# Softmax cross-entropy on one core: PSUM accumulators, new load sizes and one first transfer in place of two

## The chip, the core and the metric

The kernel runs on one core of one Trainium2 chip. The metric is the device time of one execution in microseconds; a kernel is timed in several executions and the median counts. A core has five engines with an instruction queue each: TensorE (PE, matmuls), VectorE (DVE), ScalarE (ACT, activation functions), GpSimd (POOL) and SyncE (SP, which here only issues transfers). Transfers between main memory and the on-chip memory SBUF are carried out by 16 DMA engines. Matmuls write to a second on-chip memory, PSUM.

## What is computed

For 256 rows of 32000 logits, the loss of each row against its label:

```python
log_probs = logits - np.max(logits, axis=-1, keepdims=True)
log_probs = log_probs - np.log(np.sum(np.exp(log_probs), axis=-1, keepdims=True))
return np.array([-log_probs[i, labels[i]] for i in range(batch)]).astype(np.float32)
```

Logits are float32 (32.77 MB in all), labels int32, the output 256 float32. The kernel leaves the maximum out and computes log(sum(exp(x)) * exp(-x[label])), which is the same number.

## The kernel before

**Layout.** Partition p of the 128 holds logits rows 2p and 2p + 1 one after the other, so it reads 64000 columns; "row 0" and "row 1" below are those two halves. The columns are cut into 14 loads, numbered 0 to 13, with the widths in `CHUNKS` (line 18). Loads 0 to 5 have SBUF buffers of their own (`SLOTS`, line 22), load 6 reuses load 2's, and loads 7 to 13 lie side by side in load 1's (`x_tail`, line 86). So load 6 is issued only when exp 2 is done, and loads 7 to 13 only when exp 1 is done; they stand behind load 6 in SP's queue.

**Loads.** All are issued from SP by `load` (line 110), one transfer each, except load 0, which is two transfers: the even partitions, then the odd ones (lines 114 to 116). `begin_first_load_before_barrier` (line 30) takes the first two of SP's transfers out of the kernel's body and puts them ahead of the barrier that all engines pass at the start of the program.

**Exps.** `exps` (line 120) has ScalarE compute exp of a load in place, with the sum over the columns as a second output. In the profile that is an ACTIVATE and, after it, an ACTIVATION_READ_ACCUMULATOR that writes the sum. The load in which row 0 ends (`turn`, load 3) is done in two pieces. The sums go to columns of `parts[r]` (SBUF, one column for each piece), that of load 13 to `s_last`.

**Labels.** A transfer issued from POOL brings the labels into `lbl` (line 145), POOL adds the rows' offsets (line 150), and two indirect transfers gather the logit of each label into `g` (line 152). ScalarE computes `eg` = exp(-g) between exp 2 and exp 3 (line 167), and VectorE scales the identity by it into two diagonal matrices `diag` (line 169).

**Reduction.** For each half, VectorE sums `parts[r]` into `sums` (lines 173 and 181), and a matmul of that column with `diag[r]` multiplies by exp(-g) and turns the 128 partitions into one row in PSUM, `lane[r]` (lines 174 and 182). For row 1 a second matmul adds `s_last` (line 184). A float32 matmul is two passes in the profile. ScalarE takes the logarithm (`log_row`, line 135), for row 0 after exp 4, for row 1 at the end, and one transfer stores 256 results.

**Products that nobody reads.** After exp 8 (`WARM_FROM`) TensorE computes 12 matmuls into `warm` (lines 177 to 180) that are not used for the result.

The order of the instructions on each engine is the order of the program's text (`manual_schedule`, line 140). Semaphores between engines are put in by the framework; beyond data dependences, a transfer also waits until an earlier one that used the same semaphore has landed.

Of the kernel before, what the change touches and what calls it, by code (L numbers as in the profile page):

```python
# [9 lines left out]
P = 128  # L10
ROWS = 2
F32 = mybir.dt.float32
# [3 lines left out]


CHUNKS = [
    1024, 15104, 12672, 8960, 7136, 4992, 3872,
    2848, 2144, 1600, 1216, 992, 800, 640,  # L20
]
SLOTS = [0, 1, 2, 3, 4, 5, 2]
TAIL = len(SLOTS)
TAIL_SLOT = 1

WARM_FROM = 8
WARM = 12


def begin_first_load_before_barrier(nc):  # L30


    main, body = nc.m.functions[0].blocks[:2]
    rest = list(body.instructions)
    first = [i for i in rest if i.engine == mybir.EngineType.SP and i.opcode == "DMACopy"][:2]
    for i in first:
        rest.remove(i)
    head = list(main.instructions)
    at = next(
        k for k, i in enumerate(head) if i.engine == mybir.EngineType.SP and i.opcode == "Drain"  # L40
    )
    head[at:at] = first
    main.instructions = head
    body.instructions = rest


@with_exitstack
def kernel(
    ctx: ExitStack,
    tc: tile.TileContext,  # L50
    logits: bass.AP,
    labels: bass.AP,
    out: bass.AP,
):
    nc = tc.nc
    nc.at_finalize(begin_first_load_before_barrier)
    B, C = logits.shape
    assert B == P * ROWS and sum(CHUNKS) == ROWS * C


    flat = logits.rearrange("(p r) c -> p (r c)", r=ROWS)


    pieces = []
    starts = []
    at = 0
    for n in CHUNKS:
        starts.append(at)
        cuts = [at] + [c for c in range(C, ROWS * C, C) if at < c < at + n] + [at + n]
        pieces.append([(a, b, a // C) for a, b in zip(cuts, cuts[1:])])  # L70
        at += n
    last = len(CHUNKS) - 1

    turn = next(i for i in range(len(CHUNKS)) if starts[i] + CHUNKS[i] >= C)

    big = ctx.enter_context(tc.tile_pool(name="big", bufs=1))
    small = ctx.enter_context(tc.tile_pool(name="small", bufs=1))
    psum = ctx.enter_context(tc.tile_pool(name="psum", bufs=1, space=bass.MemoryType.PSUM))

    width = {}  # L80
    for i, s in enumerate(SLOTS):
        width[s] = max(width.get(s, 0), CHUNKS[i])
    tiles = []
    for i, s in enumerate(SLOTS):
        tiles.append((big.tile([P, width[s]], F32, name=f"x{i}", tag=f"slot{s}"), starts[i]))
    tail = big.tile([P, width[TAIL_SLOT]], F32, name="x_tail", tag=f"slot{TAIL_SLOT}")
    assert sum(CHUNKS[TAIL:]) <= width[TAIL_SLOT]
    tiles += [(tail, starts[TAIL])] * (len(CHUNKS) - TAIL)

    n_of = [sum(1 for ps in pieces[:-1] for q in ps if q[2] == r) for r in range(ROWS)]  # L90
    parts = [small.tile([P, n_of[r]], F32, name=f"parts{r}") for r in range(ROWS)]
    s_last = small.tile([P, 1], F32, name="s_last")
    res = small.tile([1, ROWS * P], F32, name="res")
    sums = small.tile([P, ROWS], F32, name="sums")
    ident = small.tile([P, P], F32, name="ident")
    diag = [small.tile([P, P], F32, name=f"diag{r}") for r in range(ROWS)]
    lane = [psum.tile([1, P], F32, name=f"lane{r}") for r in range(ROWS)]
    warm = psum.tile([1, P], F32, name="warm")
    lbl = small.tile([P, 2 * ROWS], I32, name="lbl")
    idx = small.tile([P, ROWS], I32, name="idx")  # L100
    g = small.tile([P, ROWS], F32, name="g")
    eg = small.tile([P, ROWS], F32, name="eg")

    nc.scalar.preload_act_table_set("natural_log_exp_and_others")  # L104

    lbl_words = dataclasses.replace(
        labels.tensor, shape=[labels.tensor.shape[0] * 2], dtype=I32
    )

    def load(i):  # L110
        t, base = tiles[i]
        a, b = starts[i], starts[i] + CHUNKS[i]

        step = 2 if i == 0 else 1
        for p in range(step):
            nc.sync.dma_start(out=t[p:P:step, a - base:b - base], in_=flat[p:P:step, a:b])  # L116

    seen = [0] * ROWS

    def exps(i):  # L120
        t, base = tiles[i]
        for a, b, r in pieces[i]:
            if i == last:
                acc = s_last[:, :]
            else:
                acc = parts[r][:, seen[r]:seen[r] + 1]
                seen[r] += 1
            nc.scalar.activation(  # L128
                out=t[:, a - base:b - base],
                in_=t[:, a - base:b - base],  # L130
                func=AF.Exp,
                accum_out=acc,
            )

    def log_row(r):
        nc.scalar.activation(  # L136
            out=res[0:1, r:ROWS * P:ROWS], in_=lane[r][:, :], func=AF.Ln
        )

    with tc.manual_schedule():  # L140
        first = len(set(SLOTS))
        for i in range(first):
            load(i)

        nc.gpsimd.dma_start(  # L145
            out=lbl[:, :], in_=bass.AP(tensor=lbl_words, offset=0, ap=[[2 * ROWS, P], [1, 2 * ROWS]])
        )
        nc.gpsimd.iota(out=idx[:, :], pattern=[[C, ROWS]], base=0, channel_multiplier=ROWS * C)  # L148
        make_identity(nc, ident[:, :])
        nc.gpsimd.tensor_add(out=idx[:, :], in0=idx[:, :], in1=lbl[:, 0:2 * ROWS:2])  # L150
        for r in range(ROWS):
            nc.gpsimd.indirect_dma_start(  # L152
                out=g[:, r:r + 1],
                out_offset=None,
                in_=logits[:, :],
                in_offset=bass.IndirectOffsetOnAxis(ap=idx[:, r:r + 1], axis=1),
            )


        done = 0  # L160
        for i in range(first, len(CHUNKS)):
            slot = SLOTS[i] if i < TAIL else TAIL_SLOT
            while done <= SLOTS[:first].index(slot):
                exps(done)
                done += 1
            load(i)
        nc.scalar.activation(out=eg[:, :], in_=g[:, :], func=AF.Exp, scale=-1.0)  # L167
        for r in range(ROWS):
            nc.vector.tensor_scalar_mul(diag[r][:, :], ident[:, :], eg[:, r:r + 1])  # L169
        for i in range(done, last):  # L170
            exps(i)
            if i == turn:
                nc.vector.reduce_sum(out=sums[:, 0:1], in_=parts[0][:, :], axis=mybir.AxisListType.X)  # L173
                nc.tensor.matmul(lane[0][:, :], sums[:, 0:1], diag[0][:, :], start=True, stop=True)  # L174
            if i == turn + 1:
                log_row(0)
            if i == WARM_FROM:
                col = parts[1][:, seen[1] - 1:seen[1]]
                for _ in range(WARM):
                    nc.tensor.matmul(warm[:, :], col, diag[0][:, :], start=True, stop=True)  # L180
        nc.vector.reduce_sum(out=sums[:, 1:2], in_=parts[1][:, :], axis=mybir.AxisListType.X)  # L181
        nc.tensor.matmul(lane[1][:, :], sums[:, 1:2], diag[1][:, :], start=True, stop=False)  # L182
        exps(last)
        nc.tensor.matmul(lane[1][:, :], s_last[:, :], diag[1][:, :], start=False, stop=True)  # L184
        log_row(1)
        nc.sync.dma_start(
            out=out.rearrange("(a n) -> a n", a=2), in_=res[0:1, :].rearrange("o (a n) -> o a n", a=2)
        )
# [30 lines left out]
```

## Time and profile before

| what | value |
|---|---|
| median of 3 runs | 87.37 us (87.28 to 87.47) |
| the profiled execution's own time | 87.28 us |
| its span, first to last instruction | 85.5 us |
| ACT busy | 58.4 us (68% of the span) |
| PE busy | 6.1 us (7%) |
| POOL, DVE busy | 3.7 us, 0.8 us |
| read from main memory | 32.77 MB, 383 GB/s over the span |
| ACT idle until a load landed | 22.8 us in 4 waits, longest 19.8 |
| exp 1 (15104 columns) | starts at 24.64, takes 12.79 us |
| exp 13 (640 columns) | starts at 81.87, takes 0.72 us |
| last matmul pair, Ln, store issued | 82.73, 83.15, 83.45 |

Times are microseconds from the span's start. The profile gives the busy time of each engine, the chain of work that ended last, what each idle engine waited for, and for each transfer the time from its issue to its landing, that is until the last of its parts had arrived. The trace also has the records of the DMA engines' packets. A line number is that of the kernel's text.

### The profile page before, as it was taken

What the parts mean: (1) busy time and instruction counts of PE and PEld (TensorE: products, weight loads), DVE (VectorE), ACT (ScalarE), POOL (GpSimd) and SP (SyncE); (2) the same over time, 40 slices, a digit from 0 to 9 for tenths busy, and PEclk for the clock granted to TensorE, in tenths of its full rate; (3) what the DMA queues carried; (4) which work ended last, traced back from release to release, by engine and by line L of the source; (5) the groups of instructions that cost most, each with busy time, mean ns of one, the idle gap of its engine ahead of it and who ended that gap; (6) DMA issues with size and microseconds to landing.
All of it is one profiled execution on the core that took longest, in us unless ns stands there. A gap on an engine that the chain in (4) does not pass through costs nothing.

```text
span 85.5 us, 177 instructions
## 1 busy us (share of the span) xinstructions
PE 6.1 (7%) x30; PEld 3.0 (4%) x30; DVE 0.8 (1%) x4; ACT 58.4 (68%) x34; POOL 3.7 (4%) x11
## 2 busy tenths in 40 slices
PE   0000000000000000000000000200000000007980
PEld 0000000000000000000000000000000000004530
DVE  0000000000000000000000020000000000000000
ACT  1720000000049999954999999998999999999970
POOL 0600005400000000000000000000000000000000
PEclk9999999999999999999999999999999999999999
DMA  3996999999999999999989999999999999999300
GB/s 73 427 424 255 425 424 452 424 453 424 393 427 427 498 403 403 403 434 419 470 369 453 435 428 427 427 394 430 437 415 442 407 427 414 411 410 405 148 0 0
DMA packets 2131, 32.77 MB, mean 383 GB/s; under 512 B 338, under 2 KB 339, under 8 KB 1107
## 3 DMA queue, kind: packets, MB, share of 16 engines
q1 hardware_dynamic: 2034, 32.77, 90.9%
q0 software_dynamic: 96, 0.00, 0.4%
q14 instruction: 1, 0.00, 0.0%
HBM read 32.77 MB, written 0.00 MB: 383 GB/s over the span
## 4 chain that ended last, share of the span: by engine, by line
DMA 44%; ACT 38%; issue 13%; PE 0%; SPq 0%; another core or an unknown queue 0%
DMA x<-in_logits_dram 44%; ACT x L128 26%; ACT x_tail L128 12%; ACT res L136 1%; PE lane L184 0%; SPq L116 0%; ACT eg L167 0%
## 5 line engine op out<-in xcount | busy, mean ns | idle before, releaser
L128 ACT ACTIVATE x<-x 128x1024 f32<-128x1024 f32 (+7 forms) x8 | 46.4, 5794 | 22.8 <-DMA x<-in_logits_dram 22.8
L128 ACT ACTIVATE x_tail<-x_tail 128x2848 f32<-128x2848 f32 (+6 forms) x7 | 9.8, 1404 | 0.0
L180 PE MATMUL warm<-diag,parts 128*1 128x128 f32 x24 | 4.9, 392 | 23.2 <-ACT x_tail L128 23.2
L174 PE MATMUL lane<-diag,sums 128*1 128x128 f32 x2 | 0.6, 394 | 53.7 <-DVE sums L173 53.7
L180 PEld LDWEIGHTS warm<-diag,parts 128*1 128x1 f32 x24 | 2.8, 118 | 25.5 <-ACT x_tail L128 23.7
L104 ACT ACT_TABLE_LOAD x1 | 1.3, 1283 | 1.8 <-PEq L203 1.8
L152 POOL DMA_INDIRECT g<-in_logits_dram,idx x2 | 2.0, 995 | 0.6 <-issue 0.3
L174 PEld LDWEIGHTS lane<-diag,sums 128*1 128x1 f32 x2 | 0.1, 80 | 53.7 <-DVE sums L173 53.7
L128 ACT ACTIVATION_READ_ACCUMULATOR x<-x 128x1 f32 x8 | 1.5, 186 | 0.0
L128 ACT ACTIVATION_READ_ACCUMULATOR x_tail<-x_tail 128x1 f32 x7 | 1.3, 185 | 0.0
L169 DVE TENSOR_SCALAR diag<-ident,eg 128x128 f32<-128x128 f32 x2 | 0.5, 284 | 50.7 <-ACT eg L167 50.7
L136 ACT ACTIVATE res<-lane 1x128 f32<-1x128 f32 x2 | 0.5, 264 | 0.5 <-PE lane L184 0.5
L145 POOL DMA_DIRECT2D lbl<-in_labels_dram x1 | 0.7, 712 | 1.9 <-POOLq L203 1.9
L150 POOL TENSOR_TENSOR idx<-idx,lbl 128x2 int32<-128x2 int32 x1 | 0.2, 193 | 9.5 <-DMA lbl<-in_labels_dram 9.5
L181 DVE TENSOR_REDUCE sums<-parts 128x1 f32<-128x10 f32 x1 | 0.2, 164 | 28.4 <-ACT x_tail L128 28.4
L184 PE MATMUL lane<-diag,s_last 128*1 128x128 f32 x2 | 0.4, 270 | 0.1
L182 PE MATMUL lane<-diag,sums 128*1 128x128 f32 x2 | 0.4, 270 | 0.0
masks.py:199 POOL TENSOR_SCALAR_AFFINE_SELECT ident<-ident 128x128 f32<-128x128 f32 x1 | 0.3, 292 | 0.1
masks.py:197 POOL MEMSET ident<- 128x128 f32 x1 | 0.2, 232 | 0.0
L167 ACT ACTIVATE eg<-g 128x2 f32<-128x2 f32 x1 | 0.2, 187 | 0.0
L173 DVE TENSOR_REDUCE sums<-parts 128x1 f32<-128x4 f32 x1 | 0.2, 157 | 2.3 <-ACT x L128 2.3
L148 POOL IOTA idx<- 128x2 int32 x1 | 0.2, 162 | 0.1
(6 smaller groups left out, 0.6 us busy)
## 6 DMA issues: line engine op xcount, KB each, us to landing
x<-in_logits_dram SPq DMA_DIRECT2D x1, 7552.0 KB, 22.8
x<-in_logits_dram SPq DMA_DIRECT2D x1, 6336.0 KB, 37.4
x<-in_logits_dram SPq DMA_DIRECT2D x1, 4480.0 KB, 47.5
x<-in_logits_dram SPq DMA_DIRECT2D x1, 3568.0 KB, 55.5
x<-in_logits_dram SPq DMA_DIRECT2D x1, 2496.0 KB, 60.5
x<-in_logits_dram SPq DMA_DIRECT2D x1, 1936.0 KB
x_tail<-in_logits_dram SPq DMA_DIRECT2D x1, 1424.0 KB, 21.7
x_tail<-in_logits_dram SPq DMA_DIRECT2D x1, 1072.0 KB, 23.8
```

The source lines that it names most:

```text
L104: nc.scalar.preload_act_table_set("natural_log_exp_and_others")
L128: nc.scalar.activation(out=t[:, a - base:b - base], in_=t[:, a - base:b - base], func=AF.Exp, accum_out=acc,)
L136: nc.scalar.activation(out=res[0:1, r:ROWS * P:ROWS], in_=lane[r][:, :], func=AF.Ln)
L145: nc.gpsimd.dma_start(out=lbl[:, :], in_=bass.AP(tensor=lbl_words, offset=0, ap=[[2 * ROWS, P], [1, 2 * ROWS]]))
L148: nc.gpsimd.iota(out=idx[:, :], pattern=[[C, ROWS]], base=0, channel_multiplier=ROWS * C)
L150: nc.gpsimd.tensor_add(out=idx[:, :], in0=idx[:, :], in1=lbl[:, 0:2 * ROWS:2])
L152: nc.gpsimd.indirect_dma_start(out=g[:, r:r + 1], out_offset=None, in_=logits[:, :], in_offset=bass.IndirectOffsetOnAxis(ap=idx[:, r:r + 1 ...
L169: nc.vector.tensor_scalar_mul(diag[r][:, :], ident[:, :], eg[:, r:r + 1])
L174: nc.tensor.matmul(lane[0][:, :], sums[:, 0:1], diag[0][:, :], start=True, stop=True)
L180: nc.tensor.matmul(warm[:, :], col, diag[0][:, :], start=True, stop=True)
L182: nc.tensor.matmul(lane[1][:, :], sums[:, 1:2], diag[1][:, :], start=True, stop=False)
L184: nc.tensor.matmul(lane[1][:, :], s_last[:, :], diag[1][:, :], start=False, stop=True)
```

## The change

Five things are changed.

1. Load 0 is one transfer of 128 partitions again, and only this one is moved ahead of the barrier.
2. The widths of the loads are others; their number and their sum stay.
3. The sums of exps 7 to 12 go to six PSUM tiles `far` of one column each. After each of these exps VectorE copies the column to an SBUF tile `near`, and a matmul adds it into `lane[1]`. The reduction of `parts[1]` now covers the loads up to 6 and stands after exp 6. The two `lane` rows share one PSUM tile.
4. The 12 unread matmuls stand after exp 7 and take as their column one of load 7's exps in place of a sum.
5. The labels' transfer is issued from ScalarE's queue, behind the load of the function table and ahead of exp 0.

```diff
--- before.py
+++ after.py
@@ -16,15 +16,17 @@


 CHUNKS = [
-    1024, 15104, 12672, 8960, 7136, 4992, 3872,
-    2848, 2144, 1600, 1216, 992, 800, 640,
+    1024, 16384, 12512, 9024, 6656, 5088, 3744,
+    2688, 2016, 1504, 1120, 864, 736, 640,
 ]
 SLOTS = [0, 1, 2, 3, 4, 5, 2]
 TAIL = len(SLOTS)
 TAIL_SLOT = 1

-WARM_FROM = 8
+WARM_FROM = 7
 WARM = 12
+
+IN_PSUM = range(7, 13)


 def begin_first_load_before_barrier(nc):
@@ -32,14 +34,13 @@

     main, body = nc.m.functions[0].blocks[:2]
     rest = list(body.instructions)
-    first = [i for i in rest if i.engine == mybir.EngineType.SP and i.opcode == "DMACopy"][:2]
-    for i in first:
-        rest.remove(i)
+    first = next(i for i in rest if i.engine == mybir.EngineType.SP and i.opcode == "DMACopy")
+    rest.remove(first)
     head = list(main.instructions)
     at = next(
         k for k, i in enumerate(head) if i.engine == mybir.EngineType.SP and i.opcode == "Drain"
     )
-    head[at:at] = first
+    head.insert(at, first)
     main.instructions = head
     body.instructions = rest

@@ -87,14 +88,20 @@
     assert sum(CHUNKS[TAIL:]) <= width[TAIL_SLOT]
     tiles += [(tail, starts[TAIL])] * (len(CHUNKS) - TAIL)

-    n_of = [sum(1 for ps in pieces[:-1] for q in ps if q[2] == r) for r in range(ROWS)]
+    n_of = [
+        sum(1 for ps in pieces[:IN_PSUM[0]] for q in ps if q[2] == r) for r in range(ROWS)
+    ]
+    assert all(len(pieces[i]) == 1 for i in IN_PSUM) and turn < IN_PSUM[0]
+    far = {i: psum.tile([P, 1], F32, name=f"far{i}") for i in IN_PSUM}
+    near = {i: small.tile([P, 1], F32, name=f"near{i}") for i in IN_PSUM}
     parts = [small.tile([P, n_of[r]], F32, name=f"parts{r}") for r in range(ROWS)]
     s_last = small.tile([P, 1], F32, name="s_last")
     res = small.tile([1, ROWS * P], F32, name="res")
     sums = small.tile([P, ROWS], F32, name="sums")
     ident = small.tile([P, P], F32, name="ident")
     diag = [small.tile([P, P], F32, name=f"diag{r}") for r in range(ROWS)]
-    lane = [psum.tile([1, P], F32, name=f"lane{r}") for r in range(ROWS)]
+    lane_tile = psum.tile([1, ROWS * P], F32, name="lane")
+    lane = [lane_tile[:, r * P:(r + 1) * P] for r in range(ROWS)]
     warm = psum.tile([1, P], F32, name="warm")
     lbl = small.tile([P, 2 * ROWS], I32, name="lbl")
     idx = small.tile([P, ROWS], I32, name="idx")
@@ -110,10 +117,7 @@
     def load(i):
         t, base = tiles[i]
         a, b = starts[i], starts[i] + CHUNKS[i]
-
-        step = 2 if i == 0 else 1
-        for p in range(step):
-            nc.sync.dma_start(out=t[p:P:step, a - base:b - base], in_=flat[p:P:step, a:b])
+        nc.sync.dma_start(out=t[:, a - base:b - base], in_=flat[:, a:b])

     seen = [0] * ROWS

@@ -122,6 +126,8 @@
         for a, b, r in pieces[i]:
             if i == last:
                 acc = s_last[:, :]
+            elif i in IN_PSUM:
+                acc = far[i][:, :]
             else:
                 acc = parts[r][:, seen[r]:seen[r] + 1]
                 seen[r] += 1
@@ -142,7 +148,7 @@
         for i in range(first):
             load(i)

-        nc.gpsimd.dma_start(
+        nc.scalar.dma_start(
             out=lbl[:, :], in_=bass.AP(tensor=lbl_words, offset=0, ap=[[2 * ROWS, P], [1, 2 * ROWS]])
         )
         nc.gpsimd.iota(out=idx[:, :], pattern=[[C, ROWS]], base=0, channel_multiplier=ROWS * C)
@@ -174,12 +180,17 @@
                 nc.tensor.matmul(lane[0][:, :], sums[:, 0:1], diag[0][:, :], start=True, stop=True)
             if i == turn + 1:
                 log_row(0)
+            if i == IN_PSUM[0] - 1:
+                nc.vector.reduce_sum(out=sums[:, 1:2], in_=parts[1][:, :], axis=mybir.AxisListType.X)
+                nc.tensor.matmul(lane[1][:, :], sums[:, 1:2], diag[1][:, :], start=True, stop=False)
+            if i in IN_PSUM:
+                nc.vector.tensor_copy(out=near[i][:, :], in_=far[i][:, :])
+                nc.tensor.matmul(lane[1][:, :], near[i][:, :], diag[1][:, :], start=False, stop=False)
             if i == WARM_FROM:
-                col = parts[1][:, seen[1] - 1:seen[1]]
+                at = starts[i] - tiles[i][1]
+                col = tiles[i][0][:, at:at + 1]
                 for _ in range(WARM):
                     nc.tensor.matmul(warm[:, :], col, diag[0][:, :], start=True, stop=True)
-        nc.vector.reduce_sum(out=sums[:, 1:2], in_=parts[1][:, :], axis=mybir.AxisListType.X)
-        nc.tensor.matmul(lane[1][:, :], sums[:, 1:2], diag[1][:, :], start=True, stop=False)
         exps(last)
         nc.tensor.matmul(lane[1][:, :], s_last[:, :], diag[1][:, :], start=False, stop=True)
         log_row(1)
```

## The prediction

> **What bounds the kernel now.** I read the chain that ended last in order of time, then the transfers with their time to landing, the DMA rate by stage, and last the order of instructions near both ends.
>
> ```profile
> 2.25 37.36 DMA x<-in_logits_dram
> 39.62 0.02 issue
> ...
> 72.85 9.84 ACT x_tail L128 x14
> 82.69 0.04 issue
> 82.73 0.39 PE lane L184 x2
> ```
>
> The first 39.62 us are DMA, the rest is ScalarE without a pause worth naming: it looks like two bounds. The landings say it is one.
>
> ```profile
> x<-in_logits_dram SPq DMA_DIRECT2D x1, 7552.0 KB, 22.8
> x<-in_logits_dram SPq DMA_DIRECT2D x2, 256.0 KB, 3.0
> x_tail<-in_logits_dram SPq DMA_DIRECT2D x1, 320.0 KB, 17.0
> ```
>
> Load 1 was issued at 1.83 and landed at 1.83 + 22.8 = 24.62; load 13 was issued at 64.60 and landed at 81.60. Exp 13 starts at 81.87, only 0.27 after its data. So the end is the **DMA stream's end plus 0.27 us of ScalarE's lag**, plus a fixed tail (last exp, matmul pair, Ln, store).
>
> The stream is regular once it runs. Load 2 took 39.62 - 24.62 = 15.00 for 12672 columns and load 3 took 10.62 for 8960, so 4.38/3712 = 1.180 ns a column; from load 1 to load 13, 56.98 us for 47872 columns in 12 loads leave about 0.037 a load. It is not regular at its start:
>
> ```profile
> 4.00:6.00 2.00, 0.00 (x0) 0.00 (x0) 0.00 (x0) 0.83 (x2) 0.00 (x0) 1.00 0.84 302
> 6.00:8.00 2.00, 0.00 (x0) 0.00 (x0) 0.00 (x0) 0.00 (x0) 0.00 (x0) 1.00 0.98 393
> ...
> 26.00:28.00 2.00, 0.00 (x0) 0.00 (x0) 0.00 (x0) 2.00 (x1) 0.00 (x0) 1.00 0.99 431
> ```
>
> The last column is GB/s: 302 and 393 early, 431 later. The trace's packet records (start, length, bytes of each) show why. The 16 DMA engines finish load 0 at about 3.2; seven start on load 1 at once (3.08 to 3.27), the other nine at 3.87 to **4.95**. From then on each moves at its own steady pace, so load 1 lands on the first engine at 22.32 and on the last at 24.62, load 13 at 79.21 and 81.60: the late engine sets every landing. Whatever that engine gains at the start, the end gains.
>
> **Part 1, load 0 as one transfer, one issue ahead of the barrier.**
>
> ```profile
> 0.60 0.58 SPq L116 DMA_DIRECT2D x<-in_logits_dram  x1
> 1.83 0.37 SPq L116 DMA_DIRECT2D x<-in_logits_dram  x1
> ```
>
> SP reaches the barrier after its second issue. Without it the barrier, the table load and load 1's issue all come 0.60 earlier, load 1's at 1.23. Against that, one transfer has 128 rows to hand out. The packets show first rows on the engines from 1.34 to 1.90 for the first 64 rows, 0.56, and for load 1's 128 rows, which can start 1.34 after its issue (3.17), until 4.95, 1.78. If load 0's 128 rows go at the first pace (1.12), they are out by 2.46, before load 1 can start (1.23 + 1.34 = 2.57): load 1's last engine starts 0.60 earlier. At the second pace load 0 is out at 3.12 and load 1's last engine starts at 4.90: gain 0.05. Both rows describe the same unit and I have nothing to prefer one, so **-0.33**, bounds -0.60 and -0.05. Exp 0 may move either way: exp 1 waits 19.8 us.
>
> **Part 2, the labels' transfer from POOL's queue to ACT's.** On ACT it stands behind the table load and ahead of exp 0; SP's issues take 0.33 to 0.58, and exp 0's delay is covered as above. Inside the DMA engines it replaces one 128-byte packet each, 0.015 to 0.633 long, 0.58 on the latest engine (the next latest, 0.08 ahead at landing, had 0.31). Each row on SP's queue is one packet in the trace, so ACT's queue would put 8 packets of 16 bytes on each engine, between rows of load 1. The nearest row is the gather's 32-byte packets: 0.015 each between two rows, so 8 x 0.017 = 0.14. The two latest engines would gain 0.44 and 0.17, the landing 0.17 + 0.08 = 0.25. Other end: one of the eight waits the full 0.633, plus seven short ones, 0.75, a loss of 0.17. ACT's rows may also be handed out beside load 1's (rival 2), so I take **-0.15**. The labels may land as late as load 1, about 25; the index add, two gathers (1.0 each, 9.7 to landing) end near 37, and eg is read at 50.4: 13 us of cover, after which each microsecond costs one.
>
> The Trainium skill, "DMA: Bandwidth & Descriptors", section Specifications, speaks against 16-byte rows: under 512 B a transfer is read, modified and written. The 15 ns packets show no such price; no run here shows it for the labels.
>
> **Part 3, sizes and PSUM accumulators.** An exp costs, start to next start, (12789 - 10762)/2432 = 0.8335 ns a column plus 0.187: 72.76 to 75.32 for 2848. Of the 0.187, 0.093 is the accumulator's read that the next exp doesn't overlap.
>
> ```profile
> 64.75 0.19 ACT L128 ACTIVATION_READ_ACCUMULATOR x<-x 128x1 f32 x1
> 64.84 0.26 ACT L136 ACTIVATE res<-lane 1x128 f32<-1x128 f32 x1
> 65.00 4.34 ACT L128 ACTIVATE x<-x 128x4992 f32<-128x4992 f32 x1
> ```
>
> No instruction of the trace makes ScalarE write PSUM. The nearest reads it: Ln holds ScalarE 0.156 for 128 columns, so 0.049 beyond them, where the exp of 2 columns in SBUF (eg) holds it 0.094. That is 0.044 less, which I take for each of the six: 0.143 in place of 0.187. Bounds: the whole read hidden (0.094), or its full 0.185 exposed (0.28).
>
> Through load 6 exps 3 to 6 start within 0.04 of their landings (exp 3: 2080 + 6944 columns, 7.52 + 0.37 = 7.89 against load 4's 6656 x 1.181 + 0.037 = 7.90). Exp 6 needs 3.12 + 0.187 = 3.31 for a load of 3.21, so exp 7 starts 0.115 late. From there ScalarE needs 8928 x 0.8333 = 7.44 plus six overheads; loads 8 to 13 take 6880 x 1.181 + 0.22 = 8.35. At 0.143: 8.30, exp 13 is 0.07 late, against 0.27 now: **-0.20**. At 0.187: 0.33 late, +0.06. At 0.094: never under 0.02, -0.25. At 0.28: 0.89 late, +0.62. The columns moved into loads 0 and 1 cost the stream nothing: the total stays 64000.
>
> **Part 4, the sums on VectorE and TensorE.** Six copies and pairs of matmuls are spread behind exps 7 to 12. Only the last is near the path. Today the reduce (0.164, at 82.00) and its pair (0.38) end at 82.59, and the last pair waits for exp 13 until 82.73: 0.14 spare. A copy of one PSUM column instead of the reduce costs between nothing and the 128-column scaling's 0.28, +0.12: hidden, price 0. The unread products start after exp 7, about 75.3 instead of 77.44, at 0.213 a pass; passes went to 0.109 at 81.45 to 81.66, some 4.1 us after the first. So the change comes at about 79.4, and the 26 passes end near 80.1, before exp 12. Where the clock stays slow, the last pair costs 0.58 (line 174) and not 0.38.
>
> The Trainium skill, "TensorE: Matmul & The Clock Gate", section Part 1, adds that the activity window of about 3.4 us runs freely: an estimate from that page has the fast clock 3.4 to 6.8 us after the first product, 80.9 to 84.3 before and 78.7 to 82.1 after, so that some runs before end slow and hardly any after. It would take up to another 0.2 from the median; the profiled run, already fast at 82.73, shows nothing of it, and it is not in the sum.
>
> **Slot waits.** Load 6 still waits for exp 2, now near 51.1, with loads 4 and 5 queued to 65. Loads 12 and 13 wait for an earlier landing (now 58.67 and 64.58); after, load 5's at the latest, with 14 us of data queued. Free.
>
> **Sum.** 87.28 (span 85.5, 1.8 around it) - 0.33 - 0.15 - 0.20 = 86.60. The median of the runs, 87.37, lies 0.09 above the profiled one, so **86.7**.
>
> **Rivals.**
> 1. *The start gives nothing.* The stagger of one 128-row transfer eats the earlier barrier, and labels cost what they did: 87.37 - 0.20 = 87.17; with no gain from PSUM 87.43. For it: load 1's own stagger of 1.78. So 87.0 to 87.5.
> 2. *Slower: labels and load 1 share the handing out.* ACT's issue follows the barrier within 0.1 of SP's. If the 128 label rows are dealt alternately with load 1's, load 1's last engine starts up to 1.78 later: 4.95 - 0.33 + 1.78 = 6.40, +1.45; with -0.15 - 0.20, 88.5; half shared, 87.6. It decides from a last start after 5.3. Against it: load 1 is issued first.
> 3. *PSUM is dearer.* At 0.28, +0.62 - 0.48: 87.5. Against it: Ln's row.
>
> Chances: forecast 0.55 (86.2 to 87.1), rival 1 0.22, rival 2 0.15, rival 3 0.08. The best of all bounds, -0.60 - 0.25 - 0.25, gives 86.3; the range 86.1 to 87.8 leaves out the upper part of rival 2. About 0.2% (0.17 us) is what a measurement can tell from no change: faster 0.62 (the forecast and a third of rival 1), same 0.17 (half of rival 1 and of rival 3), slower 0.21 (rival 2 and the rest).
>
> **What would show it.** Load 1 issued near 1.23; its landing near 24.62 + 1.51 (1280 columns) - 0.48 = 25.65; accumulator reads into PSUM with the next exp some 0.05 behind them; exp 13 within 0.1 of its landing. A load 1 landing after 26.3 makes the forecast wrong, as does exp 13 over 0.4 late.

## The result and the profile after

The kernel after takes **84.42 us** (median of 6 runs, 84.13 to 84.65) against 87.33 (6 runs, 87.08 to 87.71) for the kernel before on the same chip: a ratio of 0.9665, 95% interval 0.9636 to 0.9693. The forecast was 86.7 with a range from 86.1 to 87.8: the sign was right, the gain is 2.9 us and not 0.6. The profiled execution took 84.65 us with a span of 82.9. (Here and below, ratios leave out disturbed runs, which the medians contain; where the kernel before had some on its chip, the two differ, by 1.3% at most, in e12.)

The chain that ended last, of the kernel after (start, length, what):

```profile
1.18 37.38 DMA x<-in_logits_dram
38.56 0.02 issue
...
71.01 9.07 ACT x_tail L134 x14
80.08 0.04 issue
80.13 0.39 PE lane L195 x2
```

It has the shape of before: DMA first, then ScalarE without a pause. DMA ends 1.06 earlier (38.56 against 39.62) although it has brought 1120 more columns by then (loads 0 to 2: 29920 against 28800, 1.32 us at 1.180 ns a column). The last matmul pair is 2.60 earlier. So 2.4 of the 2.6 are there before 39 us, and the end of the kernel, where most of the change was made, adds little.

The transfers of the kernel after (kind, count, KB where given, us from issue to landing):

```profile
x<-in_logits_dram SPq DMA_DIRECT2D x1, 22.8
x_tail<-in_logits_dram SPq DMA_DIRECT2D x1, 320.0 KB, 16.0
lbl<-in_labels_dram ACTq DMA_DIRECT2D x1, 2.0 KB, 22.9
```

The first line is load 1. It takes 22.8, as before, for 1280 columns more. Its issue and that of load 0, on SP's own rows of the kernel after:

```profile
0.00 0.40 SPq L120 DMA_DIRECT2D x<-in_logits_dram  x1
0.80 0.33 SPq L120 DMA_DIRECT2D x<-in_logits_dram  x1
```

Load 1 is issued at 0.80, 1.03 earlier than before and 0.43 earlier than forecast: one issue (0.55) and its gap (0.05) are gone, the issue that is left takes 0.40 in place of 0.58, and SP's drain behind it takes 0.12 in place of 0.37. It lands at 23.57; forecast was 25.65. With the columns' 1.51 us set aside the landing has gained 24.62 + 1.51 - 23.57 = 2.56.

The packet records of the DMA engines say where. They don't name the engine, but each row of load 1 that begins within 0.003 us of the end of an earlier packet follows it on its engine; the others begin after an idle time.

| | before | after |
|---|---|---|
| engines that go from load 0 to load 1 within 0.003 us | 7 of 16 | **16 of 16** |
| the others stand idle at least | 0.58 to 1.66 us | none |
| latest first row of load 1 | 4.95 | 3.66 |
| first rows take (the steady pace of this row length) | 2.4 to 3.0 (2.23) | 2.42 to 2.53 (2.42) |
| longest packet of the labels | 0.63 | 0.009 |

Idle time is counted here from the latest end of any packet of load 0, so it is a least value.

How the 2.56 splits can't be read off exactly, since the engines have no names. Over all 16, the first row of load 1 begins 0.78 earlier on average (3.88 to 3.10; the latest 1.29 earlier), and the rows of load 1 run over their steady pace by 0.07 an engine in place of 0.82. The labels come on top: on the two engines that end load 1 last, before, their packets take 0.58 and 0.60. If packets that join without a gap are followed, the engine that starts at 4.95 is not one of these two: its last row ends at 23.62, theirs at 24.10 and 24.17.

One view misled me. The DMA rate in two-microsecond windows, for the kernel after (last column GB/s):

```profile
2.00:4.00 2.00, 0.00 (x0) 0.00 (x0) 0.00 (x0) 0.08 (x1) 0.00 (x0) 1.00 1.73 719
4.00:6.00 2.00, 0.00 (x0) 0.00 (x0) 0.00 (x0) 1.15 (x2) 0.00 (x0) 1.00 1.14 492
6.00:8.00 2.00, 0.00 (x0) 0.00 (x0) 0.00 (x0) 0.00 (x0) 0.00 (x0) 1.00 0.92 393
```

719 is far above the steady 431, and 393 at 6 to 8 stands here too, though nothing is slow: the view counts a packet whole in the window in which it begins, and a row takes 2.42 us, longer than the window. With each packet's bytes spread over its own time, the kernel after moves 432 and 433 GB/s at 4 to 6 and 6 to 8, and the kernel before 313 and 376. So the prediction read its 302 and 393 rightly: the start of before is slow. Twelve-microsecond windows err less, though the busy share of 1.12 shows that they still do; the first twelve microseconds of before, then of after (spread in the same way, 334 and 399):

```profile
1.00:13.00 12.00, 0.00 (x0) 0.00 (x0) 0.00 (x0) 2.43 (x3) 1.31 (x4) 1.00 0.97 366
```

```profile
1.00:13.00 12.00, 0.00 (x0) 0.00 (x0) 0.00 (x0) 2.23 (x3) 0.46 (x3) 1.00 1.12 459
```

### The profile page after: what moved, and what is told of

It reads as the page before. It is cut to its first block, busy times and chain, and to the rows that moved or that the text cites. A ratio compares the mean times of both kernels' runs of the same rounds, so it can differ in the third digit from the quotient of the medians.

```text
span 82.9 us, 204 instructions
## 1 busy us (share of the span) xinstructions
PE 7.5 (9%) x42; PEld 3.7 (4%) x42; DVE 1.7 (2%) x10; ACT 58.1 (70%) x34; POOL 3.0 (4%) x10
## 4 chain that ended last, share of the span: by engine, by line
DMA 45%; ACT 38%; issue 13%; PE 0%; SPq 0%
DMA x<-in_logits_dram 45%; ACT x L134 26%; ACT x_tail L134 11%; ACT res L142 1%; PE lane L195 0%; SPq L120 0%; ACT eg L173 0%
## 5 line engine op out<-in xcount | busy, mean ns | idle before, releaser
L134 ACT ACTIVATE x<-x 128x1024 f32<-128x1024 f32 (+7 forms) x8 | 46.9, 5866 | 21.4 <-DMA x<-in_logits_dram 21.4
L134 ACT ACTIVATE x_tail<-x_tail 128x2688 f32<-128x2688 f32 (+6 forms) x7 | 9.1, 1346 | 0.0
L193 PE MATMUL warm<-diag,x_tail 128*1 128x128 f32 x24 | 4.3, 359 | 0.0
L193 PEld LDWEIGHTS warm<-diag,x_tail 128*1 128x1 f32 x24 | 2.7, 112 | 1.6
L188 PE MATMUL lane<-diag,near 128*1 128x128 f32 x12 | 2.0, 292 | 2.2 <-DVE near L187 2.2
L187 DVE COPY near<-far 128x1 f32<-128x1 f32 x6 | 0.9, 158 | 7.4 <-ACT x_tail L134 7.4
L188 PEld LDWEIGHTS lane<-diag,near 128*1 128x1 f32 x12 | 0.8, 82 | 3.3 <-DVE near L187 3.1
```

Source lines behind the costliest of these rows:

```text
L134: nc.scalar.activation(out=t[:, a - base:b - base], in_=t[:, a - base:b - base], func=AF.Exp, accum_out=acc,)
L187: nc.vector.tensor_copy(out=near[i][:, :], in_=far[i][:, :])
L188: nc.tensor.matmul(lane[1][:, :], near[i][:, :], diag[1][:, :], start=False, stop=False)
```

## The experiments

All ratios are to the kernel before on the same chip; the runs were spread over several chips. "At once" is the number of DMA engines whose first row of load 1 begins within 0.05 us of the latest end of a packet before it, so at most that many go on at once. "Idle" is the range of the others' time since that end, so they stand idle at least that long. "Latest" is the latest first row of load 1. All three are of one profiled execution; that of e1 (85.65) is the slowest of its runs, that of e11 (86.54) the fastest. On the chip of e9 to e12 the kernel before itself took 85.81 to 88.19, so small differences there say little.

| run | median (runs) | ratio, 95% | load 1 issued | at once | idle | latest |
|---|---|---|---|---|---|---|
| before | 87.33 (6) | 1 | 1.83 | 7 | 0.58-1.66 | 4.95 |
| after | 84.42 (6) | 0.9665, 0.9636-0.9693 | 0.80 | 16 | - | 3.66 |
| e1 | 84.71 (5) | 0.9716, 0.9639-0.9793 | 0.80 | 15 | 0.33 | 3.57 |
| e2 | 87.38 (10) | 1.0039, 0.9998-1.008 | 1.83 | 5 | 0.06-1.90 | 5.23 |
| e3 | 87.23 (10) | 0.9939, 0.9892-0.9986 | 1.83 | 6 | 0.58-2.35 | 5.71 |
| e4 | 84.57 (4) | 0.9712, 0.9615-0.9809 | 0.80 | 16 | - | 3.29 |
| e5 | 87.96 (10) | 1.005, 1.0015-1.0085 | 1.23 | 9 | 1.01-2.02 | 5.59 |
| e6 | 85.94 (4) | 0.9852, 0.9791-0.9913 | 1.77 | 3 | 0.09-1.21 | 4.40 |
| e7 | 84.43 (6) | 0.9658, 0.9618-0.9698 | 0.81 | 16 | - | 3.32 |
| e8 | 84.41 (6) | 0.9662, 0.9621-0.9703 | 0.81 | 16 | - | 3.43 |
| e9 | 87.21 (10) | 1.0083, 1.0022-1.0144 | 1.27 | 8 | 0.55-1.99 | 5.03 |
| e10 | 86.78 (10) | 1.0023, 0.9967-1.0078 | 1.84 | 12 | 0.22-1.00 | 4.66 |
| e11 | 87.23 (4) | 1.0126, 0.9977-1.0276 | 1.83 | 6 | 0.11-1.26 | 4.56 |
| e12 | 84.25 (4) | 0.9807, 0.9638-0.9976 | 0.80 | 16 | - | 3.12 |
| e13 | 86.75 (4) | 0.9895, 0.9829-0.9962 | 1.35 | 10 | 0.85-1.42 | 4.81 |
| e14 | 86.91 (4) | not given | 1.20 | 11 | 1.24-1.99 | 5.22 |
| e15 | 86.84 (10) | 0.9905, 0.9872-0.9938 | 1.28 | 13 | 0.70-0.80 | 4.54 |
| e16 | 87.53 (10) | 0.997, 0.9928-1.0012 | 1.48 | 6 | 0.22-2.22 | 5.66 |
| e17 | 86.20 (4) | 0.9864, 0.978-0.9949 | 1.83 | 13 | 0.09-0.63 | 5.52 |
| e18 | 85.23 (4) | 0.9748, 0.9672-0.9824 | 1.35 | 16 | - | 4.70 |

### One part at a time

**e1**, the kernel before with load 0 as one transfer, alone ahead of the barrier:

```diff
-    ... i.opcode == "DMACopy"][:2]
+    ... i.opcode == "DMACopy"][:1]
-        step = 2 if i == 0 else 1
+        step = 1
```

> The kernel before with load 0 as one transfer and one issue ahead of the barrier, nothing else. Theory T1 (issue): load 1 is issued near 0.8 in place of 1.83, its late rows are hidden behind load 0, and it lands 1.0 to 1.5 us earlier (23.1 to 23.6): 86.0. Theory T2 (labels): what holds load 1 back is POOL's transfer of the labels right behind the barrier, which is still there: late and slow first rows stay, 0.0 to 0.3 us gained, 87.1. Theory T3 (row size): load 1's rows of 60416 bytes are dealt out slower than rows of 65536 bytes and stay so: 0.0 to 0.3 us gained, 87.1.

It gives 84.71, 2.4 of the 2.9 us, with the old sizes, sums in SBUF and the labels on POOL. The labels' longest packet falls from 0.63 to 0.13 without being moved.

**e2**, before with the labels' transfer on `nc.scalar` in place of `nc.gpsimd`:

> The kernel before with the labels' transfer issued from ScalarE's queue, nothing else. T2: load 1's first rows take 2.23 us in place of 2.4 to 3.0 and the labels' packets 0.1 in place of 0.6 on the latest engine, load 1 lands 1.0 to 1.3 us earlier: 86.2. T1 and T3: only the labels' packets get cheaper, 0.2 to 0.6 us: 86.9.

**e3**, before with the `CHUNKS` of after:

> The kernel before with the widths of the kernel after, nothing else. T3: load 1 (1280 columns more, worth 1.51 us) lands near 25.0 in place of 26.1 and the end comes 1.1 us earlier: 86.3. T1 and T2: load 1 lands at 26.1, the stream ends as before, ScalarE's lag at exp 13 is 0.33 in place of 0.27: 87.4.

**e4**, after with the labels' transfer back on `nc.gpsimd`:

> The kernel after with the labels' transfer issued from POOL's queue again, nothing else. T2: 1.0 to 1.3 us are lost again: 85.6. T1 and T3: 0.2 to 0.6 us lost through the labels' packets: 84.8.

The labels cost nothing that these runs can tell on either queue, alone (e2) or with the rest (e4, whose interval is 1% wide on either side). In e4 their longest packet is 0.78, longer than before, and the time is still 84.57. The sizes alone give between 0.1 and 1.1% by the ratio, with medians that differ by 0.13 the other way: at most a fraction of what e1 gives.

**e7**, after with the accumulators in SBUF:

```diff
-    far = {i: psum.tile([P, 1], F32, name=f"far{i}") for i in IN_PSUM}
+    far = {i: small.tile([P, 1], F32, name=f"far{i}") for i in IN_PSUM}
```

> The kernel after with the six accumulators in SBUF, copies and matmuls as they are. By the prediction's term an exp then takes 0.187 and not 0.143 beyond its columns, exp 13 starts 0.33 after its landing in place of 0.12: +0.2 us, 84.6. If the shorter step from exp to exp is given back by a longer last accumulator read (0.23 in the kernel after against 0.185), +0.15 or less. Rival: the PSUM accumulators are what made the kernel faster: +1 us or more.

84.43: no gain shows in the time, but a ratio's interval of 0.4% (0.35 us) can't tell 0.2 from nothing, and the kernel after was not timed beside it. What PSUM does shows in the rows of exp 7, then of exp 13, in the kernel after:

```profile
70.92 2.43 ACT L134 ACTIVATE x_tail<-x_tail 128x2688 f32<-128x2688 f32 x1
73.25 0.15 ACT L134 ACTIVATION_READ_ACCUMULATOR x_tail<-x_tail 128x1 f32 x1
73.30 1.87 ACT L134 ACTIVATE x_tail<-x_tail 128x2016 f32<-128x2016 f32 x1
...
79.22 0.77 ACT L134 ACTIVATE x_tail<-x_tail 128x640 f32<-128x640 f32 x1
79.84 0.23 ACT L134 ACTIVATION_READ_ACCUMULATOR x_tail<-x_tail 128x1 f32 x1
80.13 0.38 PE L195 MATMUL lane<-diag,s_last 128*1 128x128 f32 x2
```

The next exp starts 0.05 behind the start of the read into PSUM (73.25 to 73.30), as forecast; from exp to exp that is 0.143 beyond the columns in place of 0.187. But the reads lengthen with each exp, from 0.150 (exp 7) to 0.192 (exp 12), and the last one, into SBUF, takes 0.230. In e7 it takes 0.18:

```profile
79.10 0.72 ACT L134 ACTIVATE x_tail<-x_tail 128x640 f32<-128x640 f32 x1
79.73 0.18 ACT L134 ACTIVATION_READ_ACCUMULATOR x_tail<-x_tail 128x1 f32 x1
```

With the sums in SBUF and the same sizes, exp 13 starts 0.38 behind its landing (e7: 78.72 to 79.10; e3 has 0.38 too), with PSUM 0.12: 0.26 less, of which about 0.04 is paid back between the start of exp 13 and the end of its read (0.85 in place of 0.81). That e7 is not slower for it is because load 13 landed 0.38 earlier in its profiled execution (78.72 against 79.10), which the sums have no part in.

**e8**, after with `WARM = 0`, so without the unread products:

> The kernel after without the 12 products that nobody reads. The last pair of matmuls runs at the slow clock, 0.58 in place of 0.38: +0.2 us, 84.6. Rival: the five pairs behind exps 7 to 12 keep TensorE busy enough, or the pair is not what ends the run: no change.

84.41. The last pair is slower, 0.58 in place of 0.38, and the runs can't tell the 0.2 from nothing:

```profile
79.67 0.58 PE L195 MATMUL lane<-diag,s_last 128*1 128x128 f32 x2
```

The products can cost time as well. In the profiled executions of e3, e5, e10 and e13 they take 5.2 to 5.3 us (3.9 to 5.1 in the others) and end so late that the last pair waits for TensorE, by 0.20 to 0.32 us beyond the usual 0.05. In e13, whose last sum is there at 81.99, the chain that ended last runs through them:

```profile
76.15 5.12 PE warm L195 x24
81.27 1.20 PE lane L190 x10
82.47 0.23 PE lane L197 x2
```

### What in "one transfer" does it

**e5**, before with three transfers ahead of the barrier (`[:3]`): load 1 is issued at 1.23, still behind both halves.

> The kernel before with load 1's issue ahead of the barrier too, behind the two halves of load 0; nothing else. Theory T1, sharpened by e1: what counts is that load 1's rows stand in the engines' queues before load 0's run out. Load 1 is issued near 1.2, no engine waits for its first row, load 1 lands near 23 and the time is 84.9, although load 0 is still two transfers and the barrier is later still. Rival T4 (the two halves themselves leave the engines apart or in a slower state): the late and slow first rows stay, 87.1.

0.5% slower, not faster (0.2 us of this, in the profiled execution, is TensorE's wait described under e8). An issue 0.6 earlier, the whole of the forecast's gain, is worth nothing here.

**e9**, before with load 0 cut by columns, 512 and 512, all 128 partitions in each:

```diff
-        step = 2 if i == 0 else 1
-        for p in range(step):
-            nc.sync.dma_start(out=t[p:P:step, a - base:b - base], in_=flat[p:P:step, a:b])
+        cut = [a, (a + b) // 2, b] if i == 0 else [a, b]
+        for lo, hi in zip(cut, cut[1:]):
+            nc.sync.dma_start(out=t[:, lo - base:hi - base], in_=flat[:, lo:hi])
```

> The kernel before with load 0 cut into two halves of its columns (128 partitions by 512) in place of even and odd partitions, both ahead of the barrier; load 1 is issued at 1.83 as before. Theory T5 (which rows go to which engine): a transfer of 64 partitions deals its rows to other engines than load 1 does, and that makes load 1's first rows late and slow. With column halves the dealing is load 1's own: as in e6 only the late issue costs, 85.9. Rival T6 (number and lateness): two transfers ahead of the barrier cost the same however they are cut: 87.2.

**e10**, before with load 0 cut into partitions 0 to 63 and 64 to 127:

> The kernel before with load 0 cut into the lower and the upper 64 partitions, both ahead of the barrier. If it is the step of two partitions that costs, this gives 86; if any transfer of 64 partitions does (T5), or any second transfer (T6), 87.2.

So neither the step of two over the partitions nor the number of rows of a transfer is the cause by itself. In e9 load 1 was issued at 1.27, not at 1.83 as the expectation has it (the issues take 0.40 and 0.41 there, the drain 0.13), so e9 is a second case of an earlier issue without a gain.

**e6**, after with load 1 made to wait for a POOL memset of 1024 of its columns:

```diff
         for i in range(first):
+            if i == 1:
+                nc.gpsimd.memset(tiles[1][0][:, 0:1024], 0.0)
             load(i)
```

> The kernel after, but load 1 waits for a POOL memset of 1024 columns of its buffer behind the barrier, which should put its issue at 1.8 to 2.2 as in the kernel before; load 0 is one transfer. T1: late and slow first rows come back, load 1 lands 2 us or more later, 86.5 to 87. T4: a delay of 1 us costs at most what the engines idle behind load 0, under 0.5 us: 84.8.

Load 1 is issued at 1.77, nearly as late as before, and about half of the gain is gone (85.94).

**e11** and **e12**, before and after with load 2 (and so loads 3 to 5) held back by a memset of 4096 of its columns, issued at 5.37 and 4.33:

> The kernel before, but load 2, and with it loads 3 to 5 behind it in SP's queue, waits for a POOL memset of 4096 columns of its buffer, to near 5.7 us. Theory T7 (issues against rows): the DMA engines run load 1's rows late and slowly as long as SP is still handing out loads 2 to 5, so with these held back load 1 starts on all engines by 3.6 with rows of 2.23: 85.5. T5 and T6: no change at load 1's start, 87.2.

> The kernel after with load 2 held back in the same way, to near 4.7 us, when all engines are within load 1's rows. T7: the rows that run from 4.7 to 7.2 get slower by 0.3 to 1 us, since loads 2 to 5 are handed out then: 84.9 to 85.3. Otherwise nothing changes, load 2 is wanted only at 22: 84.4.

In e12 load 2's issue falls into load 1's first rows, and all but two of these (2.55 and 2.78) take 2.42 to 2.44. e11 is inconclusive: its profiled run has fewer long idle times (three over 0.5), its median has not moved. e12 has the lowest median of all runs, 84.25 (84.22 to 85.36), which is not to be told from 84.42; no run beat the kernel after clearly.

### Second transfer, lateness, or engines that run dry

I then held T8, that a second transfer ahead of load 1 in SP's queue is what costs.

**e13**, as e6 with a memset of 512 columns, so that load 1 is second in the queue and issued at 1.35:

> The kernel after, load 1 waits for a short POOL memset of its first 512 columns, so that it is issued near 1.25 and not 0.80: the same time as in the kernels before whose load 1 is third in SP's queue (issued at 1.225 with three transfers ahead of the barrier, at 1.275 with column halves), but here it stands second. T8 (what costs is a second transfer that stands ahead of load 1 in the queue): the lateness of 0.45 costs at most itself, 84.4 to 84.9. T9 (what costs is load 1's issue coming too late for the engines' first free moment, whatever stands ahead): some 86.5 to 87, with last first rows near 4.5.

**e14** and **e15**, after with one more transfer between load 0 and load 1, ahead of the barrier as well, of one row or of 128 rows:

```diff
             load(i)
+            if i == 0:
+                nc.sync.dma_start(out=extra[0:1, :], in_=flat[0:1, 0:256])
```

> The kernel after with one more transfer on SP between load 0 and load 1: one row of 1 KB into a tile that nobody reads, ahead of the barrier as well. Load 1 is third in the queue and issued near 1.2. T8 with the number of transfers as the cause: 86.5 to 87.2. T8 with the rows of the second transfer as the cause (64 or 128 rows in the kernels before): like a delay of 0.4, 84.4 to 84.9.

> The kernel after with one more transfer on SP between load 0 and load 1: 128 rows of 512 bytes (64 KB, 0.15 us of the stream) into a tile that nobody reads, ahead of the barrier as well. Load 1 is third and issued near 1.25. T8, by number or by rows: 86.5 to 87.3. T9 (lateness alone): what the kernel with load 1 issued half a microsecond late gives plus 0.15. A theory that the split of load 0 itself costs: 84.6 to 85.0.

**e16**, before with the odd partitions of load 0 issued from ScalarE's queue, ahead of ScalarE's own wait at the barrier:

> The kernel before, but the odd partitions of load 0 are issued from ScalarE's queue, ahead of its own wait at the barrier; load 1 is now second in SP's queue and issued near 0.8 to 1.2. T8 (a second transfer ahead in the same queue): 84.7 to 85.2. If a second transfer costs in whatever queue it stands: 86.5 to 87.3.

**T8 falls** as the whole cause: e13 has no second transfer ahead and takes 86.75. e16 has it in another queue and takes 87.53, but its load 1 is late as well (1.48, not 0.8 to 1.2). A delay of 0.55 us, by SP's row in e13, costs 2.3 by the medians and 2.0 by the ratios; 0.26 of it, in the profiled execution, is TensorE's wait:

```profile
1.35 0.33 SPq L120 DMA_DIRECT2D x<-in_logits_dram  x1
```

e14, whose one row hardly moves data, shows how near the edge this is: three of its four runs took 86.89 to 87.00 and one 85.00 (hence no ratio).

That left the issue time by itself (T9), or what the records suggested (T10): an engine that has finished load 0 before load 1's rows have reached it runs dry and takes 0.6 to 2 us to start again. They differ if the engines are kept busy longer at an unchanged issue time. Both last kernels have load 0 of 2048 columns and take the 1024 from load 1.

**e17**, the kernel before:

```diff
-    1024, 15104, 12672, 8960, 7136, 4992, 3872,
+    2048, 14080, 12672, 8960, 7136, 4992, 3872,
```

> The kernel before with load 0 of 2048 columns in place of 1024 and load 1 of 14080 in place of 15104: still two transfers by even and odd partitions, load 1 still third in the queue and issued near 1.83. T8 (a second transfer ahead) and T9 (load 1's issue later than about 0.8) both give the kernel before, 87.0 to 87.7. T10 (a DMA engine that finishes load 0 before load 1's rows have reached it stands idle for 0.6 to 2 us, one that still has rows goes on within 0.003) says that 1.2 us more of load 0 cover this: load 1's first rows follow load 0's last at once on all or nearly all engines, 85.0 to 85.6.

**e18**, e13's kernel with `2048, 15360` in place of `1024, 16384`:

> The kernel after with load 1 issued half a microsecond late, as in the run of that name (86.75), and with load 0 of 2048 columns in place of 1024, load 1 of 15360 in place of 16384. T9 (the issue time by itself): 86.5 to 87. T10 (engines that run dry): no engine runs dry any more, 84.3 to 84.9, as if load 1 were not late.

T9's figures are out (86.5 and more for e18, 87.0 and more for e17): 85.23 and 86.20. In e18 all 16 engines go on at once and 1.5 of the 2.3 us are back (1.3 of 2.0 by the ratios, whose intervals only just part e13 from e18; e18 is also without TensorE's wait). In e17 at most 13 do, the longest idle time is at least 0.63, and half of the 2.4 us are back.

The idle time of all 16 engines together needs no names: it is the sum of the starts of those first rows of load 1 that don't follow a packet at once, less the sum of the ends that no packet follows. It falls from 9.3 us in e13 to 0 in e18, and from 11.5 in before to 2.9 in e17. The rows that begin before 8 us run over their steady pace by 0.80 an engine in e13 and 0.16 in e18, but by 0.71 in before and 0.77 in e17. So e18 changes both the idle time and the slow rows, and e17 the idle time alone; it is e17 that parts the two. Such a sum doesn't set the time by itself: in e15 it is 4.0 us, with 0.26 an engine, yet with three late engines the last row of load 1 ends at 24.93 (23.23 in the kernel after) and the time is 86.84.

The first twelve microseconds of e13, then of e18, show it too, 388 against 415 GB/s (347 against 389 with the packets spread over their time):

```profile
1.00:13.00 12.00, 0.00 (x0) 0.00 (x0) 0.00 (x0) 2.23 (x3) 3.15 (x7) 1.00 1.03 388
```

```profile
1.00:13.00 12.00, 0.00 (x0) 0.00 (x0) 0.00 (x0) 3.08 (x3) 3.16 (x7) 1.00 1.05 415
```

T10's own figures (84.3 to 84.9 and 85.0 to 85.6) were not reached. What is left is in load 1's first rows: in e17 they take 2.2 to 3.4 against a steady 2.08, even on engines that never stood idle. So **running dry is shown to be a cause and not the only one**. Load 1's rows are also shorter in e17 and e18, which no run tests by itself; the longer ones of e3 changed little. Why the first rows are slow whenever load 1 comes late, and why e6, issued later than e13, costs less than e13 (its idle times are mostly short, 11 of 13 under 0.46 since the latest end), stays open.

## Why the prediction was right and wrong

**What bounds the kernel: right.** The end is the stream's end plus a short lag: load 13 lands at 79.10 in place of 81.60, exp 13 starts at 79.22. And "whatever that engine gains at the start, the end gains" held: 2.56 at load 1's landing, 2.50 at load 13's.

**Part 1, forecast -0.33 with bounds -0.60 and -0.05: the step that failed.** The mechanism was named (SP passes the barrier earlier, load 1's latest engine starts earlier), its size was not. The prediction took the late first rows (3.87 to 4.95) as load 1's rows being handed out one after the other, so that an earlier issue could bring its own 0.60 at most. But the row it quoted from the packet records had the answer: seven engines go on at 3.08 to 3.27, and the next comes only at 3.87, after 0.58 idle. A steady handing out has no such step. The engines had run dry, and with the issue at 0.80 none does: the latest start comes 1.29 earlier (0.78 on average), and the rows' 0.75 an engine over their steady pace is gone, which had no price at all in the sum although first rows of 2.4 to 3.0 beside a steady 2.23 were in the trace. e1 puts the whole at 2.4 in time. The issue itself was mis-sized too: 0.80 and not 1.23, since the one issue of 128 rows and SP's drain behind it are shorter. Most of the gain hangs on this: e13, issued at 1.35, is 1.0% faster than before and not 3.3%, and e14, at 1.20, falls on either side. The prediction also took the engine that starts last for the one that lands last; the packets that join without a gap speak against that. The upper bound was drawn from the issue's 0.60, and that is the wrong unit: the price of missing the moment isn't the time by which it is missed (e13: 0.55 late, 2.0 to 2.3 dear; e5: 0.6 earlier but not early enough, nothing).

The Trainium skill, "DMA: Bandwidth & Descriptors", section Specifications, gives about 0.6 us from a HWDGE issue to the first byte. Load 0 agrees: its issue ends at 0.40 and its first row begins at 1.02. It speaks of the first byte alone; on the last engine of e13 load 1's first row begins at 4.81, 3.1 after the end of its issue at 1.68.

**Part 2, forecast -0.15: right in the trace, for nothing in time.** The labels' packets are 16 bytes and 0.009 each, one between two rows, and the long packet is gone. But e1 is rid of the long packet with the labels still on POOL, e4 has a longer one, and e2 and e4 find no difference. The prediction gave the next latest engine a packet of 0.31; if packets that join without a gap are followed, that engine's took 0.60, and by the prediction's own sum the landing would have gained 0.44 and not 0.25. The time knows nothing of either. The labels landed at 23.76 ("about 25"), the gathers at 36.25 ("near 37"), and eg is computed at 49.22: the cover of 13 us holds.

**Part 3, forecast -0.20: right in mechanism, the size nearer -0.10.** 0.143 an exp was exact. Exp 13 is 0.12 behind its landing, forecast 0.07, against 0.27 before: -0.15, and about 0.04 comes back behind it, which the sum didn't have. PSUM's own share is larger, 0.38 to 0.12, because the new sizes alone lengthen the lag from 0.27 to 0.38 (e3, e7; forecast 0.33). e7's time can't show a share of this size.

The Trainium skill, "ScalarE: Activation LUTs", section "Step-by-step: what each stage is for", holds PSUM for ScalarE's faster destination. The 0.143 against 0.187 agrees for the accumulator's read; e7's time can't tell whether the kernel gains by it.

**Part 4, forecast 0: right.** The reduce and its first pair are done at 71.84; the last copies and pairs lie behind exps 12 and 13. The up to 0.2 that the prediction's estimate expects of a faster last pair stands in e8's row (0.58 against 0.38), but not in its time. What the part left out is that the products themselves can hold up the last pair, by 0.20 to 0.32 us (e3, e5, e10, e13); in the profiled run of the kernel after they don't.

**Slot waits, median:** free, as said; the profiled run lies 0.23 above the median this time. None of the rivals came: rival 2's point of decision, a last start after 5.3, is far from 3.66. By the shares that the prediction names, same would have had 0.15 and slower 0.23, not 0.17 and 0.21.

## What to carry to other kernels

When a small first transfer bridges the time until a large one, look in the packet records whether each DMA engine goes from one to the other without a gap; a gap may cost several times the delay that caused it (0.55 us late, 2.0 to 2.3 us lost in e13), and what helps is a large transfer issued earlier or a first transfer that lasts longer. A row that is slower than its own steady pace is a term of the sum even when its cause isn't known. And don't read a rate from windows shorter than the packets counted in them.

## What the runs showed of the hardware

- In the kernel after all 16 DMA engines go from one transfer to the next within 0.003 us. Engines that ran dry took at least 0.06 (e2) to 2.35 us (e3) to their next row.
- In the kernels with such gaps, rows at 3 to 8 us take up to 3.46 against a steady 2.42 (e13) or 3.78 against 2.23 (e5), and up to 3.11 in e5 on engines that had none. One row is that slow without any gap as well: 3.41 against 2.27 in e18.
- SP's issues ahead of the barrier take 0.55 to 0.58 for transfers of 64 rows and 0.40 to 0.42 for 128 rows, and its drain behind them 0.37 and 0.12 to 0.13 (before, e10, e16 against after, e9, e15). In e5 a third issue, of 128 rows behind two of 64, takes 0.60.
- The accumulator's read lengthens from exp to exp when it writes PSUM, 0.150 to 0.192 over six, and the SBUF read behind them takes 0.230 against 0.185 in e7. Without PSUM the reads stay at 0.185 to 0.187 (e7).
